# Which partition takes which run of tokens: a weighted sum of two expert outputs on one core

## The chip, the core and the metric

The kernel runs on one core of a Trainium2 chip. The metric is the device time of one execution in microseconds, here the median of three runs. The profile is of one such execution; its span counts from the first to the last recorded instruction, so it is a little shorter than the device time.

## What is computed

Each of 16 x 1024 = 16384 tokens has two expert outputs of 512 float32 values and two weights. The result is their weighted sum.

```python
batch, seq, hidden, n_experts, k = 16, 1024, 512, 8, 2
# expert_outputs: (batch, seq, k, hidden) float32; combine_weights: (batch, seq, k) float32

def reference(expert_outputs, combine_weights):
    weights = combine_weights[..., np.newaxis]
    return np.sum(expert_outputs * weights, axis=2).astype(np.float32)
```

A token's two expert outputs lie side by side in HBM, 4 KB in all; its result is 2 KB. So 67.1 MB are read and 33.55 MB written, apart from the small weights.

## The kernel before

The 16384 tokens are dealt to the 128 partitions of SBUF, 128 tokens to each. The first 121 tokens of a partition are one run of consecutive tokens (121 x 4 KB = 484 KB of input), processed as 11 tiles of 11 tokens; the last 7 come from a second region at the end of the tensors, where each partition has a run of 7.

```python
P = nc.NUM_PARTITIONS            # 128
per = n // P                     # 128 tokens for each partition
J, LAST = 11, 7
main = per - LAST                # 121
eo = expert_outputs.rearrange("b s k h -> (b s) (k h)")
cw = combine_weights.rearrange("b s k -> (b s) k")
o = out.rearrange("b s h -> (b s) h")

def rows(x):
    a = x[0 : P * main, :].rearrange("(p t) f -> p t f", p=P)
    b = x[P * main : n, :].rearrange("(p t) f -> p t f", p=P)
    return lambda t, c: a[:, t : t + c, :] if t < main else b[:, t - main : t - main + c, :]

eo, cw, o = rows(eo), rows(cw), rows(o)
```

All weights are loaded once, in two transfers. Then for each tile one transfer on the sync engine's queue brings 11 tokens for all partitions into one of four buffers. VectorE multiplies them by their weights (one instruction over both experts) and adds the two halves; the sum goes into the front of the same buffer, and the scalar engine's queue stores it.

```python
ipool = ctx.enter_context(tc.tile_pool(name="in", bufs=4))
# ... cut: the weights' two transfers
for g in range(last + 1):
    et = ipool.tile([P, J, k * h], dt)
    ot = et.rearrange("p j f -> p (j f)")[:, 0 : J * h].rearrange("p (j f) -> p j f", f=h)
    t0, c = g * J, J if g < last else LAST
    nc.sync.dma_start(out=et[:, 0:c], in_=eo(t0, c))
    if g < last - 1:
        wb = wt[:, g * J * k : (g + 1) * J * k].unsqueeze(2).to_broadcast([P, J * k, h])
        ek = et.rearrange("p j (k h) -> p (j k) h", k=k)
        nc.vector.tensor_tensor(out=ek, in0=ek, in1=wb, op=mult)
        nc.vector.tensor_tensor(out=ot, in0=et[:, :, 0:h], in1=et[:, :, h : 2 * h], op=add)
        nc.scalar.dma_start(out=o(t0, c), in_=ot)
        continue
    # ... cut: the last two tiles share the multiplication between ScalarE and VectorE
    nc.sync.dma_start(out=o(t0, c), in_=ot[:, 0:c])
```

A buffer is free for its next load once its store has been read out.

Of the kernel before, what the change touches and what calls it, by code (L numbers as in the profile page):

```python
# [1 line left out]

# [4 lines left out]


@with_exitstack
def kernel(  # L10
    ctx: ExitStack,
    tc: tile.TileContext,
    expert_outputs: bass.AP,
    combine_weights: bass.AP,
    out: bass.AP,
):

    nc = tc.nc  # L20
    b, s, k, h = expert_outputs.shape
    assert k == 2
    n = b * s
    P = nc.NUM_PARTITIONS
    per = n // P
    assert per * P == n
    J, LAST = 11, 7
    main = per - LAST
    assert main % J == 0
# [3 lines that stand above are left out]

    def rows(x):

        a = x[0 : P * main, :].rearrange("(p t) f -> p t f", p=P)
        b = x[P * main : n, :].rearrange("(p t) f -> p t f", p=P)
        return lambda t, c: a[:, t : t + c, :] if t < main else b[:, t - main : t - main + c, :]

    eo, cw, o = rows(eo), rows(cw), rows(o)  # L40

    dt = mybir.dt.float32
    mult = mybir.AluOpType.mult
    add = mybir.AluOpType.add
    copy = mybir.ActivationFunctionType.Copy

    last = main // J

    wpool = ctx.enter_context(tc.tile_pool(name="w", bufs=1))
    ipool = ctx.enter_context(tc.tile_pool(name="in", bufs=4))  # L50

    wt = wpool.tile([P, per * k], dt)

    for eng, t, c in ((nc.sync, 0, main), (nc.scalar, main, LAST)):
        eng.dma_start(  # L55
            out=wt[:, k * t : k * (t + c)].rearrange("p (t k) -> p t k", k=k), in_=cw(t, c)
        )

    warm = wpool.tile([P, 1], dt)
    nc.scalar.activation(out=warm, in_=nc.const_aps.tensor(1.0, (P, 1), dt), func=copy)  # L60
# [17 lines that stand above are left out]
        for i in range(c):  # L78
            t = t0 + i
            nc.scalar.activation(  # L80
                out=et[:, i, 0:h], in_=et[:, i, 0:h], func=copy, scale=wt[:, 2 * t : 2 * t + 1]
            )
            if g == last:
                nc.vector.scalar_tensor_tensor(  # L84
                    out=ot[:, i, :],
                    in0=et[:, i, h : 2 * h],
                    scalar=wt[:, 2 * t + 1 : 2 * t + 2],
                    in1=et[:, i, 0:h],
                    op0=mult,
                    op1=add,  # L90
                )
        if g < last:
            w1 = wt.rearrange("p (t k) -> p t k", k=k)[:, t0 : t0 + c, 1:2]
            x1 = et[:, :, h : 2 * h]
            nc.vector.tensor_tensor(out=x1, in0=x1, in1=w1.to_broadcast([P, c, h]), op=mult)  # L95
            nc.vector.tensor_tensor(out=ot, in0=et[:, :, 0:h], in1=x1, op=add)  # L96
        nc.sync.dma_start(out=o(t0, c), in_=ot[:, 0:c])


# [1 line left out]
_INS = ['expert_outputs', 'combine_weights']  # L101
_OUTS = [((16, 1024, 512), 'float32')]


# [23 lines left out]
```

## Time and profile before

| | |
|---|---|
| device time, median of 3 (lowest to highest) | 239.48 us (239.21 to 240.85) |
| span of the profiled execution | 237.4 us |
| VectorE busy | 195.7 us |
| ScalarE busy | 12.7 us |
| one multiplication over 11 tokens (VectorE) | 11.89 us, 10 of them |
| one addition over 11 tokens (VectorE) | 6.03 us |
| read from HBM, written to HBM | 67.24 MB, 33.55 MB |
| first multiplication starts | 17.29 us |
| last store issued | 227.4 us |

In the profile L67 is the line that loads a tile, L72 and L73 the multiplication and the addition, L74 the store, L80, L84 and L95 to L97 the last two tiles. `et` is the tile, `wt` the weights. PE, DVE, ACT, POOL and SP are the five engines (DVE is VectorE, ACT is ScalarE); "SPq" and "ACTq" stand for the sequencers that issue transfers. Both of them hand their transfers to the same 16 DMA engines, and the page lists what each queue's packets took as a share of these engines' time in the span. Every transfer is broken into packets[...].

### The profile page before, as it was taken

How to read it: one execution, taken by the hardware profiler on the slowest of the kernel's cores; microseconds unless marked ns; L12 is line 12 of the kernel's file. 1: busy time of each engine (PE TensorE's matmuls, PEld its weight loads, DVE VectorE, ACT ScalarE, POOL GpSimd, SP SyncE). 2: the span in 40 equal slices, each digit the busy share in tenths (PEclk: the TensorE clock that was granted, in tenths of full speed). 3: DMA queues.
4: the chain of work that ended last, by engine and by line, in shares of the span. 5: the costliest groups of instructions: out<-in, count | busy, mean ns of one | idle time of the engine just before them, and what ended most of it. 6: DMA issues, size and time to landing. Idle time of an engine off the chain costs nothing.

```text
span 237.4 us, 157 instructions
## 1 busy us (share of the span) xinstructions
DVE 195.7 (82%) x29; ACT 12.7 (5%) x20; POOL 0.2 (0%) x4
## 2 busy tenths in 40 slices
DVE  0009999999999999999996996997999699689530
ACT  2000000000000000000000000000000000290600
POOL 0000000000000000000000000000000000000000
DMA  7989899989999899899989999989989999999997
GB/s 265 486 364 486 387 463 425 425 364 486 418 433 486 364 425 486 372 463 440 486 364 425 425 425 440 516 380 425 486 364 486 425 395 456 411 444 431 425 425 309
DMA packets 3744, 100.80 MB, mean 425 GB/s; under 512 B 544, under 2 KB 672, under 8 KB 672
## 3 DMA queue, kind: packets, MB, share of 16 engines
q1 hardware_dynamic: 2160, 71.95, 70.7%
q10 hardware_dynamic: 1584, 28.84, 28.3%
HBM read 67.24 MB, written 33.55 MB: 425 GB/s over the span
## 4 chain that ended last, share of the span: by engine, by line
DMA 55%; DVE 38%; ACT 1%; issue 0%; DVEq 0%; ACTq 0%; SPq 0%
DMA et<-in_expert_outputs_dram 28%; DMA out_dram<-et 27%; DVE et L72 25%; DVE et L73 13%; ACT et L80 1%; DVE et L84 0%; DVEq L123 0%; ACTq L123 0%; SPq L55 0%; SPq L67 0%; DVEq L72 0%; ACTq L80 0%
## 5 line engine op out<-in xcount | busy, mean ns | idle before, releaser
L72 DVE TENSOR_TENSOR et<-et,wt 128x11264 f32<-128x11264 f32 x10 | 118.9, 11888 | 25.2 <-DMA et<-in_expert_outputs_dram 25.2
L73 DVE TENSOR_TENSOR et<-et 128x5632 f32<-128x5632 f32 x10 | 60.3, 6025 | 0.3
L80 ACT ACTIVATE et<-et,wt 128x512 f32<-128x512 f32 x18 | 11.2, 708 | 212.0 <-DMA et<-in_expert_outputs_dram 212.0
L95 DVE TENSOR_TENSOR et<-et,wt 128x5632 f32<-128x5632 f32 x1 | 6.0, 6025 | 2.1 <-DMA et<-in_expert_outputs_dram 2.1
L84 DVE SCALAR_TENSOR_TENSOR et<-et,wt 128x512 f32<-128x512 f32 x7 | 4.9, 747 | 3.2 <-ACT et L80 3.0
L96 DVE TENSOR_TENSOR et<-et 128x5632 f32<-128x5632 f32 x1 | 6.0, 6024 | 0.8 <-ACT et L80 0.8
L60 ACT ACT_TABLE_LOAD x1 | 1.3, 1283 | 1.2 <-PEq L112 1.2
L60 ACT ACTIVATE warm<-const-float32-1.0 128x1 f32<-128x1 f32 x1 | 0.2, 203 | 0.0
L112 POOL MEMSET const-bfloat16-1.0<- 128x1 bf16 x1 | 0.1, 102 | 0.0
L112 POOL MEMSET const-uint8-127<- 128x1 uint8 x1 | 0.1, 101 | 0.0
L112 POOL MEMSET const-float32-0.0<- 128x1 f32 x1 | 0.1, 99 | 0.2 <-issue 0.2
L112 POOL MEMSET const-float32-1.0<- 128x1 f32 x1 | 0.1, 98 | 0.0
## 6 DMA issues: line engine op xcount, KB each, us to landing
et<-in_expert_outputs_dram SPq DMA_DIRECT2D x11, 5632.0 KB, 27.4
out_dram<-et ACTq DMA_DIRECT2D x10, 2816.0 KB, 30.7
et<-in_expert_outputs_dram SPq DMA_DIRECT2D x1, 3584.0 KB, 22.6
out_dram<-et SPq DMA_DIRECT2D x1, 2816.0 KB, 13.0
out_dram<-et SPq DMA_DIRECT2D x1, 1792.0 KB, 9.1
wt<-in_combine_weights_dram SPq DMA_DIRECT2D x1, 121.0 KB, 2.1
wt<-in_combine_weights_dram ACTq DMA_DIRECT2D x1, 7.0 KB, 2.3
```

What stands on the lines that cost most here:

```text
L60: nc.scalar.activation(out=warm, in_=nc.const_aps.tensor(1.0, (P, 1), dt), func=copy)
L72: nc.vector.tensor_tensor(out=ek, in0=ek, in1=wb, op=mult)
L73: nc.vector.tensor_tensor(out=ot, in0=et[:, :, 0:h], in1=et[:, :, h : 2 * h], op=add)
L80: nc.scalar.activation(out=et[:, i, 0:h], in_=et[:, i, 0:h], func=copy, scale=wt[:, 2 * t : 2 * t + 1])
L84: nc.vector.scalar_tensor_tensor(out=ot[:, i, :], in0=et[:, i, h : 2 * h], scalar=wt[:, 2 * t + 1 : 2 * t + 2], in1=et[:, i, 0:h], op0=mul ...
L95: nc.vector.tensor_tensor(out=x1, in0=x1, in1=w1.to_broadcast([P, c, h]), op=mult)
L96: nc.vector.tensor_tensor(out=ot, in0=et[:, :, 0:h], in1=x1, op=add)
L112: nc = _bacc.Bacc("TRN2", target_bir_lowering=False, num_devices=1)
```

## The change

The same tokens form the same runs, but a run goes to another partition. The 128 runs are numbered in the order in which they lie in HBM. Before, partition p takes run p. After, partition 4c+r takes run 32r+c, with c from 0 to 31 and r from 0 to 3. Partitions 0, 4, 8, ... then hold runs 0, 1, 2, ..., and the four partitions of a group hold runs that lie 32 runs apart. Inputs, weights and outputs are all dealt in this way, so that the sum of every token lands where it belongs. The aim is that neighbouring groups of four partitions read neighbouring runs in HBM.

```diff
     def rows(x):
 
-        a = x[0 : P * main, :].rearrange("(p t) f -> p t f", p=P)
-        b = x[P * main : n, :].rearrange("(p t) f -> p t f", p=P)
-        return lambda t, c: a[:, t : t + c, :] if t < main else b[:, t - main : t - main + c, :]
+        a = x[0 : P * main, :].rearrange("(r c t) f -> c r t f", r=4, t=main)
+        b = x[P * main : n, :].rearrange("(r c t) f -> c r t f", r=4, t=LAST)
+        return lambda t, c: (
+            a[:, :, t : t + c, :] if t < main else b[:, :, t - main : t - main + c, :]
+        )
```

Tile sizes, buffers, queues and arithmetic stay as they are. On the HBM side a transfer's outermost size is now 32, with 4 below it; on the SBUF side it is still 128 partitions.

## The prediction

> **What bounds the kernel now.** I read the page from its second and third parts, then the waits of the vector engine and of the sync engine's DMA queue, then a table of stretches of the span. The question of the first reading is whether any DMA engine is ever free.
>
> ```profile
> span 237.4 us, 157 instructions
> ...
> DVE 195.7 (82%) x29; ACT 12.7 (5%) x20; POOL 0.2 (0%) x4
> ...
> DMA packets 3744, 100.80 MB, mean 425 GB/s; under 512 B 544, under 2 KB 672, under 8 KB 672
> ...
> q1 hardware_dynamic: 2160, 71.95, 70.7%
> q10 hardware_dynamic: 1584, 28.84, 28.3%
> ```
>
> The two queues together keep the 16 DMA engines occupied for 70.7% + 28.3% = 99.0% of the span. VectorE is at 82%. The DMA engines are the bound, and what they carry is fixed: every input byte once (67.24 MB) and every output byte once (33.55 MB). The next view, the table of stretches, has the columns stretch, its length, busy time of DVE, ACT and POOL with instruction counts, the clock, the DMA share and GB/s.
>
> ```profile
> 5.00:17.00 12.00, 0.00 (x0) 0.00 (x0) 0.00 (x0) 1.00 1.00 432
> ...
> 35.00:88.00 53.00, 52.90 (x7) 0.00 (x0) 0.00 (x0) 1.00 0.99 423
> ...
> 119.00:200.00 81.00, 72.92 (x9) 0.00 (x0) 0.00 (x0) 1.00 0.99 429
> ```
>
> From 5 to 17 us only loads run, VectorE does nothing yet, and the engines move 432 GB/s. Later, with loads and stores mixed and VectorE busy, the rate is 423 to 429. So mixed traffic already runs within 2% of pure reading[...]. The waits say the same from the other side (engine, line, awaited: us in total, times, longest):
>
> ```profile
> DVE et L72 <- DMA et<-in_expert_outputs_dram: 25.2, 5, 17.3
> ...
> SPq L67 <- DMA out_dram<-et: 178.8, 8, 41.8
> ```
>
> VectorE idles 17.3 us for the first tile and then about 2 us for each of four later ones (25.2 - 17.3 = 7.9): in the second half it is the one that waits for data. The 178.8 us in which the load queue waits for stores to free one of the four buffers look large, but cost nothing: the engines stay 99% occupied with what is already queued. The chain of waits gives DMA 55% and VectorE 38%; I do not conclude from it that VectorE bounds 38% of the time, because the engines are full in those stretches too.
>
> **Where a floor lies.** 100.80 MB at the 432 GB/s of the pure load stretch takes 233.3 us. Nothing moves before the first issue of a large load at 1.16 us (timeline), and nothing in the last 1.4 us (a stretch from 236.0 to 237.4 answers 0 GB/s). 233.3 + 1.2 + 1.4 = 235.9 us, against a span of 237.4. All that a better order of reading could give is therefore about 1.5 us, or 0.6%. For 2% of 239.48, 4.8 us would have to go.
>
> [...] No view here shows which engine carried which partition.
> [...]
>
> **The change, part by part.**
> 1. *Instructions.* None is added, removed or moved. The comparison of the two instruction orders has the same rows on every engine; only the HBM side of a transfer is now 32x4 runs where it was 128. VectorE keeps its 195.7 us.
> 2. *Packets.* The page has 11+10+1+1+1+1+1 = 26 issues and 3744 packets, 144 for each: 128, one per partition, and 16 more. A full load is 5632 KB, so each partition gets 44 KB in one piece. After the change a partition still reads 11 consecutive tokens, 44 KB, of its run. I expect 3744 packets and 100.80 MB again: 0 us.
> 3. *Issue cost.* A load issue takes 328 ns and a store issue 339 on its queue (medians of those lines). One more dimension may add a little; only the last store's issue lies on the path, so even a doubling is 0.35 us. I take 0.1.
> 4. *Which addresses are read together.* [...] I expect -1.5 to 0 us if collisions get fewer, 0 if they do not matter; I choose -0.3, because the loss of 1.5 us also has the start-up in it, which no order removes.
> 5. *The end.* The last store carries 1792 KB and lands 9.1 us after its issue. Its shape in time stays: 0 us.
>
> Sum: 0 + 0.1 - 0.3 = -0.2, so 239.48 becomes **239.3 us**.
>
> **Rivals.**
> - *The engines are dealt differently.* The outermost size on the HBM side is now 32, on the SBUF side 128. [...] If all traffic fell to half of 432, 100.80 MB would take 467 us; if it collided about half of the time, my estimate is 300 to 350. [...]
> - *HBM collisions.* [...]
> - *The change heals collisions that I do not see.* Its limit is the floor: 239.48 - 1.5 = 238.0. This is the way in which the change would be a small gain.
> - *VectorE becomes the bound.* Against it: its work is unchanged, and it already waits. If loads landed sooner, its own limit is 17.3 + 195.7, plus the last store's 9.1 and the 1.4 at the end = 223.5 us, well below the span.
>
> **Range and chances.** The bulk, about 0.8, is the same time within the spread of before (239.21 to 240.85) and the 1.5 us that could be won, stretched upward for a small loss to collisions: 238.0 to 243.0. About 0.13 goes to differently dealt engines, far above the range, and 0.07 to collisions in HBM over 2%. Faster by over 2% would need the engines to exceed the highest rate seen in pure loading; I give it 0.01. So faster 0.01, same 0.79, slower 0.20.
>
> **What the profile after would show.** Right: 3744 packets, queue shares that add up to 99%, about 432 GB/s from 5 to 17 us, first tile computed from about 17.3 us, VectorE at 195.7 us. Dealt differently: the first load lands far later than its 16.0 us, the stretch from 5 to 17 us near half of 432, and VectorE waits tens of us for every tile, with the packet count unchanged. HBM collisions: the pure load stretch near 432 or a few per cent less, and the mixed stretches below 423. More packets than 3744 would mean that the runs are cut into shorter pieces, which would refute step 2. The prediction is wrong mainly if the share of an engine, and not the address in HBM, is what the change moves.

## The result, and the profile after

The changed kernel takes **240.91 us** (median of 6, 240.58 to 241.42) against 239.45 us (median of 6, 239.21 to 240.85). The ratio is 1.0054, with a 95% interval of 1.0029 to 1.0079: slower, by 1.3 us by the ratio and 1.5 us between the medians, and well under the 2% that the prediction asked about.

The page of the changed kernel, its parts 1 to 3:

```profile
span 239.2 us, 157 instructions
...
DVE 195.8 (82%) x29; ACT 12.7 (5%) x20; POOL 0.2 (0%) x4
...
DMA packets 3744, 100.80 MB, mean 421 GB/s; under 512 B 544, under 2 KB 672, under 8 KB 672
...
q1 hardware_dynamic: 2160, 71.95, 70.3%
q10 hardware_dynamic: 1584, 28.84, 28.0%
```

Instructions, packets and bytes are as before; VectorE has its 195.8 us. The share of the DMA engines falls from 99.0% to 98.3% of a span that is 1.8 us longer. The engines have had a little more empty time, so the next reading asks where. The table of stretches (columns as before the change: stretch, length, the engines' busy time, clock, DMA share, GB/s), first of the kernel before:

```profile
17.00:30.00 13.00, 12.68 (x2) 0.00 (x0) 0.00 (x0) 1.00 1.02 440
...
100.00:200.00 100.00, 91.85 (x12) 0.00 (x0) 0.00 (x0) 1.00 1.01 434
```

and of the changed kernel:

```profile
17.00:30.00 13.00, 11.17 (x1) 0.00 (x0) 0.00 (x0) 1.00 1.02 440
...
100.00:200.00 100.00, 91.73 (x11) 0.00 (x0) 0.00 (x0) 1.00 1.00 433
```

Once it runs, the stream has the same rate: 440 and 434 GB/s before, 440 and 433 after. The start is another matter. The chain of waits in order of time (start us, length us, what) begins before with

```profile
0.73 0.38 SPq L55
1.11 0.05 issue
1.16 16.03 DMA et<-in_expert_outputs_dram
```

and after with

```profile
0.73 0.67 SPq L58
1.40 0.05 issue
1.45 17.28 DMA et<-in_expert_outputs_dram
```

The first line is the sync engine's sequencer issuing the weights: 0.67 instead of 0.38 us. The first tile's load is therefore issued 0.29 us later. Then it needs 17.28 instead of 16.03 us, 1.25 more. The two terms make 1.54 us, and the first multiplication starts at 18.83 instead of 17.29 us. The other 0.2 us arise in later waits for buffers and loads. The end adds nothing that shows: the last store is issued at 229.19 instead of 227.43 us, already 1.76 us later, and from there it is about 10.0 us to the end in both kernels.

Every transfer has become slower to issue. Lines for the transfers of `et` in the trace (columns: line, engine, operation, count, then ns smallest/median/largest), first of the kernel before:

```profile
L67 SPq DMA_DIRECT2D et<-in_expert_outputs_dram x12: 327/328/522, 1.2 to 198.9; - x12
L74 ACTq DMA_DIRECT2D out_dram<-et x10: 338/339/342, 35.3 to 206.7; - x10
```

and of the changed kernel:

```profile
L70 SPq DMA_DIRECT2D et<-in_expert_outputs_dram x12: 534/535/929, 1.4 to 201.4; - x12
L77 ACTq DMA_DIRECT2D out_dram<-et x10: 546/547/594, 36.8 to 208.5; - x10
```

Where the 1.25 us come from can be seen in stretches of half a microsecond. A packet of a load (5632 KB / 128 = 44 KB) counts where it starts, and one such start in 0.5 us reads as 90 GB/s. Before:

```profile
2.10:2.60 0.50, 0.00 (x0) 0.49 (x2) 0.00 (x0) 1.00 4.92 1433
2.60:3.10 0.50, 0.00 (x0) 0.05 (x1) 0.00 (x0) 1.00 0.57 180
```

After:

```profile
2.60:3.10 0.50, 0.00 (x0) 0.31 (x2) 0.00 (x0) 1.00 3.39 946
3.10:3.60 0.50, 0.00 (x0) 0.00 (x0) 0.00 (x0) 1.00 1.13 360
3.60:4.10 0.50, 0.00 (x0) 0.00 (x0) 0.00 (x0) 1.00 0.31 90
4.10:4.60 0.50, 0.00 (x0) 0.00 (x0) 0.00 (x0) 1.00 0.31 90
4.60:5.10 0.50, 0.00 (x0) 0.00 (x0) 0.00 (x0) 1.00 0.25 90
```

1433 GB/s in half a microsecond is 14 starts and some of the weights' small packets, and the next stretch has the other two: before, all 16 first large packets start within a microsecond. After, nine start in the first of these stretches (beside the rest of the weights), four in the next, and then one in each of the following three, which again makes 16. The last start some 2 us after the first, in a load that takes 1.25 us longer.

**The times of the kernel before fall into two groups**, and this bears on every ratio below. Over the three chips of the experiments, 63 of its 115 executions took up to 240.21 us and the other 52 took 240.39 us or more; typical times are 239.5 and 240.9 us, as far apart as the kernel before and the changed kernel are. In the comparison above five of six executions of the kernel before lie in the lower group; no execution of the changed kernel does.

### The profile page after: what moved, and what is told of

Read it like the earlier page. It is cut to its first block, busy times and chain, and to the rows that moved or that the text cites. A ratio compares the mean times of both kernels' runs of the same rounds, so it can differ in the third digit from the quotient of the medians.

```text
span 239.2 us, 157 instructions
## 1 busy us (share of the span) xinstructions
DVE 195.8 (82%) x29; ACT 12.7 (5%) x20; POOL 0.2 (0%) x4
## 2 busy tenths in 40 slices
DMA packets 3744, 100.80 MB, mean 421 GB/s; under 512 B 544, under 2 KB 672, under 8 KB 672
## 4 chain that ended last, share of the span: by engine, by line
DMA 55%; DVE 38%; ACT 1%; issue 0%; DVEq 0%; SPq 0%; ACTq 0%
DMA out_dram<-et 28%; DMA et<-in_expert_outputs_dram 27%; DVE et L75 25%; DVE et L76 13%; ACT et L83 1%; DVE et L87 0%; DVEq L126 0%; SPq L58 0%; ACTq L126 0%; SPq L70 0%; DVEq L75 0%; ACTq L83 0%
```

## The experiments

Three assumptions of the author's about the cause, for the runs to tell apart. **Theory A:** the HBM side described as 32x4 runs makes a transfer slower to issue and slower to reach all engines; where the runs lie in HBM does not matter, and only the start (and, slightly, the last store) is on the path. **Theory B:** reads of the runs in their new order collide in HBM, at the start above all. **Theory C:** all 26 issues cost something throughout.

Ratios below are to the kernel before on the same chip. On the chip of runs 1 to 4 it took 240.67 us (median of 57, 239.26 to 241.55; 24 of them in the lower group), on that of runs 5 and 6 and of `r8` 239.56 us (30 of 43 in the lower group), on that of `r2` and run 8 239.54 us (9 of 15). A median jumps when the balance of the groups tips, so the quotient of two medians can differ from the ratio given by one or two tenths of a per cent.

**1. The description of the change with nearly the addresses of before** (`loads_gap`). With one token of gap after every fourth run, the runs no longer lie at equal distances, so that 128 plain rows can't describe them. Some tokens read are others than the reference's; stores are plain (`_n` marks the new form of a tensor, `_p` the plain one).

```diff
+        a = x[0 : 32 * (4 * main + 1), :].rearrange("(c u) f -> c u f", c=32)
+        a = a[:, 0 : 4 * main, :].rearrange("c (r t) f -> c r t f", r=4)
# ... cut: the last 7 tokens in the same way; the plain form stays beside it
-    eo, cw, o = rows(eo), rows(cw), rows(o)
+    eo, cw, o = eo_n, cw_n, o_p
```

> Stores stay as before the change. Loads and weights are described as 32x4 runs, but in nearly the order of before: partition 4c+r reads from token 485c+121r, one token of gap for each c, so that the description can't be merged back into 128 rows (a few tokens read are not those of the reference, the amount is the same). Theory A (the 32x4 description makes every transfer slower to issue and the first load slower to get going; addresses do not matter): as the changed kernel, ratio 1.004 to 1.006, load issue 535 ns, weights' issue 0.67 us, first multiplication at 18.5 to 19 us. Theory B[...]: addresses are those of before, so ratio 1.000 to 1.001 and first multiplication at 17.3 to 17.6 us even if an issue takes longer.

Measured: ratio 1.0039 (1.0022 to 1.0055), load issue 535 ns, the weights' issue 0.61 us, first multiplication at 18.39 us. All 18 executions took 240.53 us or more. The runs lie as before but for the gaps, and the loss is there. Theory B is not needed for it.

**2. Only the start in the new form** (`first_changed`). The sums of tile 0 then land at other tokens, and in the later tiles tokens meet the weights of others.

```diff
-    eo, cw, o = rows(eo), rows(cw), rows(o)
# ... cut: the new and the plain form of each tensor
+    eo = lambda t, c: (eo_n if t == 0 else eo_p)(t, c)
+    cw, o = cw_n, o_p
```

> The kernel before, with the weights and the first tile's load alone in the new form; the other loads and all stores as before (so tile 0 is computed from other tokens than the reference's). Theory A: the whole loss lies before the first multiplication, so it is all here: ratio 1.004 to 1.006, first multiplication at 18.8 us. Theory B, if collisions go on through the run: less than half of the loss, ratio 1.001 to 1.003. Theory C (all issues together cost, 26 x 0.2 us spread over the run): ratio near 1.001.

Measured: 1.0038 (1.0019 to 1.0056), all 16 executions at 240.49 us or more, first multiplication at 18.22 us. Three transfers, the weights' two and the first load, bring a loss like that of run 1, where all loads were new; the other loads and all stores were plain. The start itself varies: the changed kernel has the same three transfers and its first multiplication 0.6 us later.

**3. All but the start in the new form** (`first_plain`), the opposite of the last: `eo` plain for tile 0 and new otherwise, weights plain, stores new.

> The changed kernel, with the weights and the first tile's load alone in the form of before (tile 0 is computed from other tokens than the reference's). Theory A: the start is healed, first multiplication at 17.3 us; what is left is the last store's longer issue, 0.24 us, so ratio 1.000 to 1.002. Theory B or C: most of the loss stays, ratio 1.003 to 1.005.

Measured: 0.9996 (0.9972 to 1.0020), first multiplication at 17.53 us. Loads (median 535 ns) and stores (547 ns) still take longer to issue, and it costs nothing that shows; the interval leaves room for 0.5 us. Theory C falls, and so does theory B for the running stream: ten full loads in the new order cost nothing measurable. Six of the 14 executions lie in the lower group.

The profiled one does not: it took 241.08 us, with the early start of the kernel before. Its chain shows where this execution of the upper group loses its time. Two lines of the kernel before, whose profiled execution is of the lower group (239.17 us):

```profile
88.86 30.08 DMA out_dram<-et
164.49 34.32 DMA out_dram<-et
```

and the same waits in `first_plain`:

```profile
89.10 31.77 DMA out_dram<-et
166.38 34.32 DMA out_dram<-et
```

The 0.24 us at 89 us are the later start. One wait, for a store to free a buffer, then lasts 1.69 us longer, and all that follows is later by about as much. A 44 KB packet of a load takes about as long, an estimate from the 432 GB/s of 16 engines: 45056 x 16 / 432000 = 1.67 us. So it may be one packet's turn more or less; that is not shown. The slow start adds to this rather than being the same thing: in the profile of run 2 (241.8 us) this wait lasts 31.77 us too, after a start 0.93 us later than before.

**4. Only the stores in the new form** (`stores_changed`): `eo` and `cw` plain, `o` new, so that the sums land at other tokens.

> The kernel before, with the stores alone in the new order (the sums land at other tokens than the reference's). Theory A: store issue 547 instead of 339 ns, hidden but for the last one, so 0.2 to 0.3 us: ratio 1.000 to 1.002, start unchanged at 17.3 us. Theory B for writes[...]: ratio 1.003 or more, the loss seen in the stretches after 35 us.

Measured: 1.0001 (0.9981 to 1.0020), first multiplication at 17.32 us, ten of 22 executions in the lower group. The last store's longer issue, about a quarter of a microsecond, is below what these runs resolve.

**5. Only the weights in the new form** (`weights_changed`), `eo` and `o` plain.

> The kernel before, with the weights' two transfers alone in the 32x4 form (most tokens get other tokens' weights). If the loss is the sum of a later issue and a slower start of the first load, this shows the first term alone: the weights' issue takes 0.65 instead of 0.38 us, the first load is issued 0.27 us later, first multiplication at 17.5 to 17.7 us, ratio 1.000 to 1.002. If the whole loss came from the weights (their 968-byte pieces in scattered order delaying the first load's packets), first multiplication at 18.3 us or later and ratio 1.004.

Measured: first multiplication at 17.58 us, the 0.29 us of the later start; ratio 1.0004 (0.9982 to 1.0027). Ten of the 14 executions still lie in the lower group, with a median of 239.84 us against 239.48 for that group of the kernel before. The larger part of the late start is thus the first load's own: 18.22 us in run 2 against 17.58 here, the same kernels but for that one load.

**6. The start taken off the weights** (`early_before`, `early_after`). In both kernels, the weights are issued on the scalar engine's queue, so that the sync engine begins with the first tile.

```diff
-    for eng, t, c in ((nc.sync, 0, main), (nc.scalar, main, LAST)):
+    for eng, t, c in ((nc.scalar, 0, main), (nc.scalar, main, LAST)):
```

> The kernel before, with both transfers of the weights issued on the scalar engine's queue, so that the sync engine's first issue is the first tile's load, at 0.73 instead of 1.16 us. If the start is on the path that sets the end: first multiplication at 16.8 to 17.0 us, ratio 0.997 to 0.999. If the transfers are held up elsewhere: ratio 1.000, first multiplication at 17.2 us or later.

> The changed kernel, with both transfers of the weights issued on the scalar engine's queue. The first load is issued at 0.73 instead of 1.45 us, which takes the weights' longer issue off the path and leaves the slower start of the first load. First multiplication at 17.9 to 18.2 us; ratio to the kernel before 1.000 to 1.003. If the longer issue of the weights were the whole loss: first multiplication at 16.9 us, ratio 0.997 to 0.999.

Measured: `early_before` 239.42 us, ratio 0.9970 (0.9954 to 0.9986), the one version with a ratio clearly below 1; `early_after` 240.46 us, 1.0021 (1.0001 to 1.0040). The ratios came as expected, the first multiplication did not: 17.36 and 19.44 us instead of about 16.9 and 18.0. The waits of VectorE in `early_before` tell why (engine, line, awaited: us in total, times, longest):

```profile
DVE et L72 <- DMA wt<-in_combine_weights_dram: 17.4, 1, 17.4
DVE et L72 <- DMA et<-in_expert_outputs_dram: 7.9, 4, 2.0
```

VectorE now waits for the weights, which travel beside the first loads. The gain of `early_before` lies in the groups: all 22 executions are in the lower one, whose median in the kernel before, 239.48 us on this chip, it hardly betters. Why the upper group does not occur is not shown. `early_after`, whose multiplication starts later than in any other version with r=4, has a smaller ratio than the changed kernel, though the intervals overlap. This suggests that the start of the DMA stream counts for more than that of VectorE; these runs do not separate the two.

**7. Other group sizes** (`r2`, `r8`), the changed kernel with `r=2` and `r=8`. These ask the rival of the prediction, that the engines are dealt other partitions.

> The changed kernel with r=2: partition 2c+r takes run 64r+c, an HBM side of 64x2 runs. [...] first multiplication at 18.3 to 19 us, load issue 535 ns, ratio 1.003 to 1.007. If any second dimension other than four rows breaks the dealing: like r=8, ratio 1.3 or more.

> The changed kernel with r=8: partition 8c+r takes run 16r+c, so an HBM side of 16x8 runs, all inputs and outputs dealt alike. If what matters is that the HBM side has a second dimension: as the changed kernel, load issue 535 ns, ratio 1.003 to 1.008. If with groups of eight the engines are dealt eight consecutive partitions each[...]: first multiplication near 30 us, the stretch from 5 to 17 us near 216 GB/s, ratio 1.2 to 1.9.

Measured: `r2` 240.92 us, 1.0041 (1.0017 to 1.0065), with the slow start of the changed kernel (18.76 us). `r8` 372.85 us (median of 6), with the first multiplication at 33.1 us. Its times vary more than those of the others, from 365 to 393 us: the ratio of 1.5291 (1.5176 to 1.5407) is that of the two fastest runs, the profile that of the slowest. Stretches of that profile:

```profile
5.00:15.00 10.00, 0.00 (x0) 0.00 (x0) 0.00 (x0) 1.00 1.05 216
5.00:17.00 12.00, 0.00 (x0) 0.00 (x0) 0.00 (x0) 1.00 0.96 199
```

The DMA engines are as busy as ever (the DMA share next to the last column is about 1) and move half as much, so each packet takes about twice as long: 45056 x 16 / 216000 = 3.34 us by the estimate of run 3, where 432 GB/s gave 1.67.

**8. Why r=8 is slow** (`loads_gap8`, `halves`). The first is run 1 with 16x8 in the place of 32x4. The second is the kernel before with each load cut into partitions 0 to 63 and 64 to 127.

```diff
-        nc.sync.dma_start(out=et[:, 0:c], in_=eo(t0, c))
+        for p in (0, P // 2):
+            nc.sync.dma_start(out=et[p : p + P // 2, 0:c], in_=eo(t0, c)[p : p + P // 2])
```

> Loads and weights described as 16x8 runs, but in nearly the order of before (partition 8c+r reads from token 969c+121r; some tokens read are not those of the reference), stores as before. If r=8 is slow because of how the partitions are dealt to the engines, the loads are as slow here: first multiplication at 31 to 34 us, 5 to 17 us near 200 to 216 GB/s. If r=8 is slow because of its addresses in HBM: first multiplication at 18 to 19 us and ratio near 1.004.

> The kernel before, with every load split into two transfers, partitions 0 to 63 and then 64 to 127. All else, addresses included, as before. [...] the pure load stretch falls to about half: 5 to 17 us at 200 to 225 GB/s, first multiplication at 31 to 34 us. If the two halves overlap[...]: 425 to 432 GB/s and first multiplication near 17.5 us.

Measured: `loads_gap8` 384.01 us, 1.602 (1.596 to 1.608), first multiplication at 32.2 us; `halves` 384.39 us, 1.604 (1.596 to 1.611), first multiplication at 32.1 us; two executions each. Stretch of `loads_gap8`:

```profile
5.00:17.00 12.00, 0.00 (x0) 0.00 (x0) 0.00 (x0) 1.00 1.07 222
```

and of `halves`:

```profile
5.00:17.00 12.00, 0.00 (x0) 0.00 (x0) 0.00 (x0) 1.00 1.07 222
```

So r=8 is slow with nearly the addresses of before as well, and a transfer that is known to reach 64 partitions only has the same rate to the last digit, 222 GB/s. Whether the two are slow for the same reason is not shown: which engine had which partition is in no view.

## Why the prediction was right in its size and wrong in its reasons

- **The range held**: 240.91 lies between 238.0 and 243.0, within 2% as given 0.79. The point, 239.3, had the wrong sign: -0.2 against about +1.4 us. That the range reached far enough up was luck: it was stretched upward for collisions in HBM, and these are not what came.
- **The step that failed is the third, the issue cost.** It had 0.1 us, on the ground that only the last store's issue lies on the path. An issue did take longer, by 207 ns on 328; but the path begins with one too. The weights' issue stands ahead of the first load and gave 0.29 us. A second part was missing from the step altogether: the first load, in the new form, also reaches all its engines later and took 1.25 us longer. Together they are 1.54 of the 1.76 us by which the last store is late. The last store's issue, the one place where the step looked, shows nothing. The first-tile sign given for "right" (17.3 us) came out at 18.83 and pointed at just this.
- **The fourth step, -0.3 us from addresses, is not found.** Runs 1 and 2 with their different addresses both give about 1.004, and run 3 with the new addresses in the stream gives 0.9996. Neither gain nor collision shows; an effect of 0.2% either way could hide in these intervals.
- **Steps 1, 2 and 5 held**: 157 instructions, 3744 packets, the last store landing 9.1 us after its issue.
- **The spread of before was taken for noise.** 239.21 to 240.85 us in three executions were already the two groups, and the second is as far off as what was to be predicted.
- **The rival of the differently dealt engines** is not seen with r=4, but r=8 behaves like it: half of the load rate, and 372.85 us is between the estimate for partial collisions (300 to 350) and that for all traffic (467). Measured from 5 to 17 us: 443 and 421 GB/s with r=2 and r=4, 199 with r=8 and 222 with `halves`. Why is not shown; that the engines are dealt other partitions was the author's assumption.
- **The HBM rival** did not come about: 433 GB/s in the stream against 434. The 421 GB/s from 5 to 17 us, where 432 was the sign for "right", are three packet starts fewer in that window; `r2` and run 1, which start late too, have 443.
- **The floor** of 235.9 us for the span seemed to leave 1.5 us to win by a better order. It lets the data flow from 1.16 us on, when the first large load is issued, but the stretches before the change show its packets starting only after 2.1 us. So about 1 us of the 1.5 was never there to win (an estimate from these two times), and the new order won nothing.

## What to carry to other kernels

In a kernel that keeps the DMA engines full, count the issues ahead of the first large load, and look at how long that load takes to get all engines going: here the whole loss that could be measured lay there, and the same longer issues later in the stream cost nothing that shows. The second dimension on the HBM side made a load slower to issue here, 535 ns instead of 328, so use the plain form for what comes first. Of the groups tried, two and four rows kept the full rate (443 and 421 GB/s from 5 to 17 us, against 432 before) and eight halved it (199); a DMA share of about 1.0 with half the GB/s is the sign to look for. And run the kernel before often enough to see whether its times fall into groups, before a difference of 0.5% is given a cause.

## What the runs showed of the hardware that was not expected

- A transfer with 32x4, 64x2 or 16x8 runs on the HBM side takes 535 to 537 ns to issue as a load (medians), against 328 with 128 rows. Among these three forms the medians are within 2 ns of each other. The loads of `halves`, 64 rows with no second dimension, took longer still: 588 ns (median).
- The first large packets of the 16 engines, which started within a microsecond before (14 of them in half of one), spread over about 2 us in the changed kernel, and over somewhat more than 1 us in run 2. Why they spread, and whether the slower issue is the reason, is not shown.
- Weights issued beside the first loads landed much later. In `early_before` the weights (968 bytes for each partition) took 16.6 us from issue to landing, against 2.1 us when they were issued first; the second transfer, 56 bytes for each partition and issued about half a microsecond after the first, took 29.6. The difference of 13.0 us is about the time of eight 44 KB packets, by the estimate of 1.67 us for one. What held the weights up is not shown.
